# Smaller batches for the overflow slots of a mixture of experts, one branch for its general path, and an earlier place for it

## The chip, the cores and the metric

The kernel runs on one core of one Trainium2 chip. The metric is the device time of one execution in microseconds (us), as the median over several runs; lower is better.

## The reference, cut to what matters

Two blocks run one after the other on 256 tokens of 1024 values, all in float32. The first has a gated linear attention layer with a dense feed-forward layer, then a stick-breaking attention layer with a mixture of experts; the second has two hybrid attention layers. The change lies in the mixture of experts:

```python
def moe_swiglu(h, w_router, w_gate, w_up, w_down):
    logits = (h @ w_router).astype(jnp.float32)
    top_val, top_idx = lax.top_k(logits, TOP_K)          # 2 of 8
    top_w = jax.nn.softmax(top_val, axis=-1)
    gates = jnp.sum(jax.nn.one_hot(top_idx, N_EXPERTS) * top_w[..., None], axis=-2)
    out = jnp.zeros_like(h)
    for e in range(N_EXPERTS):
        y = (jax.nn.silu(h @ w_gate[e]) * (h @ w_up[e])) @ w_down[e]
        out = out + gates[..., e:e + 1] * y
    return out
```

`w_gate[e]` and `w_up[e]` are 1024 x 3584, `w_down[e]` is 3584 x 1024.

## The kernel before

The program is one instruction list for each engine, with no loops on the chip. A Python planner writes it: `spawn` and `after` put side work (generators) on a list, `tick` advances each by one step, and `until` and `drain` tick until a condition holds or until no side work is left. So the Python order is the order of each engine's queue.

**Weights.** `order` lists every weight chunk in order of use. `load_more` (L308) issues the next load on SP's queue (L322) for each slot in the list `free`; `let_go` (L333) puts the slots of used chunks back and calls `load_more`. A load waits on the chip until the last reader of its slot is done. In the mixture of experts there are 4 + 6 general slots, two named `extra`, and two more (`T..h`, `T..l`) that serve until the chunk `moe_g6_0_0` is reached in `order`: 14 in all, each for one chunk.

**Routing.** `route` computes the logits, ranks them, counts positions with small matmuls, sets `over_i` (has the expert more than 64 tokens?) and `most_i` (the largest count), builds the one-hot selection `pick` (`pick_pair`) and the scaled input `xs`, and `gather` then collects the tokens of two experts at a time into `xe`. TensorE also clears the bank `po` once before (L1404).

**Experts.** `moe_steps` has 16 steps, (e, g) for expert e and half g of its 3584 columns. Each expert has 64 slots for tokens, 32 further ones (`BEYOND`), and a general path for more. A step does `up` for the gate and for the up weights (8 chunks each), then `down` of the step before (7 chunks). A pass of `up` multiplies its 8 chunks by the 64 slots (L1240). Then `beyond` (L1213 on, the branch is at L1220) runs the same chunks for the 32 further slots (L1249) only if the expert's flag is set; the flag is a register on TensorE alone. Only after that are the 8 slots of the chunks let go. `down` does the same in batches of four and three (L1300, L1311). `scatter` adds the result to `X`, with matmuls for the further slots (L1199) in every case.

**General path.** `second(e2, first)` runs an expert for tokens past 96, with its own weight loads on SP. It stands in two branches (L1415), one for `first` 96 and one for 224, each over eight experts, ahead of step (6, 1). It is not taken with these inputs. It uses the two `T` slots as buffers, and `drain` runs ahead of it.

**After the last step**, `down` of step (7, 1) and its `scatter` start the norms of the hybrid layer (`TwoNorms`), and `pump` splits the first weight parts of that layer into a high and a low part (ScalarE L353, VectorE L359).

Of the kernel before, what the change touches and what calls it, by code (L numbers as in the profile page):

```python
# [16 lines left out]
P = 128  # L17
# [94 lines left out]
def whole(ctx, tc, T, out, tap):  # L112
# [919 lines left out]
    with tc.tile_pool(name="moe", bufs=1) as pool:  # L1032
# [23 lines left out]
        def route():  # L1056
            lp = yield from grab("y")
            for k in range(KT):
                while k // 4 not in norm.done:
                    yield  # L1060
                mm3(lp[0:NE, 0:S], sl(wr, ALL, k), sl(xT, ALL, k), k == 0, k == KT - 1)
                if k % 4 == 3:
                    yield
            lT = ring.tile([NE, S], F32, tag="wlo", name="lT", bufs=LA + 1)
            V.tensor_copy(lT, lp[0:NE, 0:S])
            for tt in range(2):
                nc.tensor.transpose(lp[:, S + tt * NE:S + (tt + 1) * NE], lT[:, toks(tt)], ident[0:NE, 0:NE])
            yield
            V.tensor_copy(flat(lg), lp[:, S:S + 2 * NE])
            drop(lp)  # L1070

            rank = pool.tile([P, 2, NE], F32, name="rank")
            gt, eq = (ring.tile([P, 2, NE, NE], F32, tag="wlo", name=n, bufs=LA + 1) for n in ("gt", "eq"))
            other = [lg[:, tt, :].unsqueeze(1).to_broadcast([P, NE, NE]) for tt in range(2)]
            mine = [lg[:, tt, :].unsqueeze(2).to_broadcast([P, NE, NE]) for tt in range(2)]
            for tt in range(2):
                V.tensor_tensor(eq[:, tt], other[tt], mine[tt], ALU.is_equal)
            for tt in range(2):
                V.tensor_tensor(gt[:, tt], other[tt], mine[tt], ALU.is_gt)
            V.tensor_mul(eq, eq, C("low").rearrange("p (a b) -> p a b", a=NE).unsqueeze(1).to_broadcast([P, 2, NE, NE]))  # L1080
            V.tensor_add(gt, gt, eq)
            V.tensor_reduce(rank, gt, AX.X, ALU.add)
            V.tensor_scalar(sel, rank, 2.0, None, op0=ALU.is_lt)
            yield
            ps = yield from grab("y")
            mm(ps[:, 0:NE], C("pos_tri"), sel[:, 0, :], start=True, stop=True)
            mm(ps[:, NE:2 * NE], C("pos_tri"), sel[:, 1, :], start=True, stop=False)
            mm(ps[:, NE:2 * NE], ones, sel[:, 0, :], start=False, stop=True)
            mm(ps[:, 2 * NE:3 * NE], ones, sel[:, 0, :], start=True, stop=False)
            mm(ps[:, 2 * NE:3 * NE], ones, sel[:, 1, :], start=False, stop=True)  # L1090

            over = pool.tile([P, NE], F32, name="over")
            V.tensor_scalar(over, ps[:, 2 * NE:3 * NE], SLOTS + 0.5, None, op0=ALU.is_gt)
            V.tensor_copy(over_i, over)
            counted.append(over_i)
            while not norm.ready:
                yield
            for tt in range(2):
                V.tensor_scalar(lg[:, tt, :], lg[:, tt, :], rstd[:, tt:tt + 1], None, op0=ALU.mult)
            for j in range(2):  # L1100
                for tt in range(2):
                    act(xs[0][:, tt, cols(j)], X[:, tt, cols(j)], AF.Copy, scale=rstd[:, tt:tt + 1])
                if j == 0:
                    V.tensor_copy(flat(pos), ps[:, 0:2 * NE])
                    pick_pair(0)
                else:
                    act(gates_, gates_, AF.Exp)
                for tt in range(2):
                    V.scalar_tensor_tensor(xs[1][:, tt, cols(j)], X[:, tt, cols(j)], rstd[:, tt:tt + 1], xs[0][:, tt, cols(j)], ALU.mult, ALU.subtract)
                if j == 0:  # L1110

                    top = pool.tile([P, 2], F32, name="top")
                    V.tensor_reduce(top, lg, AX.X, ALU.max)
                    V.tensor_tensor(gates_, lg, top.unsqueeze(2).to_broadcast([P, 2, NE]), ALU.subtract)
                    spawn(gather(0, 1))
                yield

            most = pool.tile([P, 1], F32, name="most")
            V.tensor_reduce(most, ps[:, 2 * NE:3 * NE], AX.X, ALU.max)
            drop(ps)  # L1120
            V.tensor_copy(most_i, most)
            yield 2
            V.tensor_mul(gates_, gates_, sel)
            gsum = pool.tile([P, 2], F32, name="gsum")
            V.tensor_reduce(gsum, gates_, AX.X, ALU.add)
            V.reciprocal(gsum, gsum)
            V.tensor_mul(gates_, gates_, gsum.unsqueeze(2).to_broadcast([P, 2, NE]))
# [51 lines left out]
        def scatter(e, y, z, nxt, ring_):  # L1179
# [8 lines left out]
            for tt in range(2):  # L1188
# [3 lines left out]
                    pbs[tt, half] = take_bank(ring_)  # L1192
                for half in range(2):
                    r = slice(half * 64, half * 64 + 64)
                    mm(pbs[tt, half], pT[r, 0, toks(tt)], ys[r, :], start=True, stop=False)
                for i in range(2):
                    for half in range(2):
                        r = slice(half * 64, half * 64 + 64)
                        mm(pbs[tt, half][:, i * 256:i * 256 + 256], pT[r, 1 + i, toks(tt)], zs[r, :], start=False, stop=i == 1)  # L1199
                yield  # L1200
                if not nxt:
                    for half in range(2):
# [23 lines left out]
        def up(e, g, n):  # L1226


            xe = xes[e // 2]
            c0 = e % 2 * P  # L1230
            mine, more_ = slice(c0, c0 + SLOTS), slice(c0 + SLOTS, c0 + SLOTS + BEYOND)
            pss = [bank("w"), bank("w")]
            ws = []
            for k in range(KT):
                until(lambda: done_k.get(e // 2, 0) > k)
                ws.append(chunk_at(f"moe_{n}{e}_{g}_{k}"))
                w_ = ws[-1][1][:, 0, :]
                for ps, a, b in ((pss[0], 0, 512), (pss[1], 512, QUART)):
                    for half in range(2):
                        mm(ps[half * 64:half * 64 + 64, 0:b - a], xe[:, k, mine], w_[:, half * QUART + a:half * QUART + b],  # L1240
                           start=k == 0, stop=k == KT - 1)
                tick()
            until(lambda: not in_po)
            in_po.append((e, g, n))

            def work():
                for k, (_, w_) in enumerate(ws):
                    for q in range(4):
                        mm(po[q * 32:q * 32 + 32, :], xe[:, k, more_], w_[:, 0, QCOL[q]:QCOL[q] + 512], start=k == 0, stop=k == KT - 1)  # L1249
            beyond(e, work)  # L1250
            let_go(i for i, _ in ws)
            tick()
            return pss

        hTs, ys, scattered = {}, {}, set()
# [68 lines left out]
        def second(e, first):  # L1324
# [21 lines left out]
            for g in range(ED // 512):  # L1346
                gu = []
                for ww in ("moe_w_gate", "moe_w_up"):
                    o = bank("fg")
                    for c in range(2):  # L1350
                        wf = raw_weights([P, 4, 512])
                        nc.sync.dma_start(wf, chunk(T[ww][0, e], c * 512, 4, g * 512, 512))
                        for kk in range(4):
                            mm(o, x2[:, c * 4 + kk, :], wf[:, kk, :], start=c + kk == 0, stop=c * 4 + kk == KT - 1)
                    gu.append(o)
# [7 lines left out]
                V.tensor_copy(flat(hT), ps)  # L1363
                for c in range(2):
                    wf = raw_weights([P, 2, D])
                    nc.sync.dma_start(wf, chunk(T["moe_w_down"][0, e], g * 512 + c * 256, 2, 0, D))
                    for kk in range(2):
                        for half in range(2):
                            i = c * 2 + kk
# [30 lines left out]
        spawn(route(), 0)  # L1400
        tick()
        po, in_po = bank("o"), []
        for q in range(4):
            mm(po[q * 32:q * 32 + 32, :], zeros, X[:, 0, 0:512], start=True, stop=True)  # L1404

        until(lambda: 0 in xes)
        free.extend((cpool, f"T{(t_at[0] + 1) % 2}{x}", order.index("moe_g6_0_0")) for x in "hl")
        load_more()
        prev = None
        for e, g in moe_steps:  # L1410
            if (e, g) == (NE - 2, 1):
                drain()
                most_v = nc.values_load(most_i[0:1, 0:1], min_val=0, max_val=S)
                for first in (SLOTS + BEYOND, SLOTS + BEYOND + P):
                    with tc.If(most_v > first):  # L1415
                        for e2 in range(NE):
                            second(e2, first)
            if (e, g) == (NE - 1, 0):
                spawn(spread_gain())
            if g == 0 and e % 2 and e < NE - 1:  # L1420
# [56 lines left out]
        rings["l"], ring_at["l"] = [7, 4, 5, 6], 0  # L1477
        norm = TwoNorms(cpool, [hT0], "n", [fg], DELAYS["hyb0"])
        down(*prev, norm.start)
        until(lambda: NE - 1 in scattered)  # L1480
        pump(st["pos"])
    more.close()
    if tap("moe", X):
        return
# [352 lines left out]
```

## Time and profile before

| | |
|---|---|
| median of 3 runs | 2048.58 us (2047.46 to 2048.61) |
| profiled execution, its own time | 2047.97 us |
| its span | 2046.2 us |
| TensorE busy in the span | 1944.7 us |
| HBM read | 532.91 MB |

The profile is of one execution. The span runs from the first to the last instruction; 1.8 us lie around it. The mixture of experts takes the span from about 424 to 1345 us. Rows name an engine, a line of the kernel and a tile; PE is TensorE, PEld its weight load, DVE VectorE, ACT ScalarE, SP the engine that issues the loads; a name with q is the engine's own sequencer.

### The profile page before, as it was taken

What the parts mean: (1) busy time and instruction counts of PE and PEld (TensorE: products, weight loads), DVE (VectorE), ACT (ScalarE), POOL (GpSimd) and SP (SyncE); (2) the same over time, 40 slices, a digit from 0 to 9 for tenths busy, and PEclk for the clock granted to TensorE, in tenths of its full rate; (3) what the DMA queues carried; (4) which work ended last, traced back from release to release, by engine and by line L of the source; (5) the groups of instructions that cost most, each with busy time, mean ns of one, the idle gap of its engine ahead of it and who ended that gap; (6) DMA issues with size and microseconds to landing.
All of it is one profiled execution on the core that took longest, in us unless ns stands there. A gap on an engine that the chain in (4) does not pass through costs nothing. (4 is left out here: it accounts for less than half of the span.)

```text
span 2046.2 us, 27694 instructions
## 1 busy us (share of the span) xinstructions
PE 1944.7 (95%) x11238; PEld 1245.4 (61%) x11238; DVE 840.1 (41%) x1678; ACT 671.4 (33%) x1161; POOL 3.7 (0%) x11
## 2 busy tenths in 40 slices
PE   8999999988888889999999899889999999999998
PEld 7889999953233223443333333267877888787886
DVE  5665557631010101010100102065677666667765
ACT  5554446530000000000010000055565645556553
POOL 0000000000000000000000000000000000000000
PEclk9999999989999999999999899999999999999999
DMA  7486554329999999999997599974444555444552
GB/s 239 137 287 210 190 186 163 127 102 416 418 417 419 417 417 408 390 373 416 417 410 302 230 408 385 391 246 141 140 144 150 180 185 168 141 145 138 171 177 80
DMA packets 179685, 536.22 MB, mean 262 GB/s; under 512 B 11186, under 2 KB 52530, under 8 KB 179524
## 3 DMA queue, kind: packets, MB, share of 16 engines
q1 hardware_dynamic: 175392, 531.66, 68.7%
q10 hardware_dynamic: 4132, 2.33, 0.5%
q8 instruction: 111, 1.82, 0.4%
q14 instruction: 50, 0.41, 0.1%
HBM read 532.91 MB, written 1.05 MB: 261 GB/s over the span
## 5 line engine op out<-in xcount | busy, mean ns | idle before, releaser
L359 DVE TENSOR_TENSOR wlo<-raw,whi 128x1024 fp32r<-128x1024 f32 x338 | 412.8, 1224 | 273.1 <-PE psw L387 125.0
L353 ACT CAST whi<-raw 128x1024 fp32r<-128x1024 f32 x338 | 354.0, 1049 | 376.9 <-PE psw L388 239.8
L1240 PE MATMUL psw<-raw,xe 128*64 128x512 f32 (+1 forms) x2048 | 413.9, 548 | 42.7 <-DMA raw<-in_moe_w_up_dram 15.7
L1240 PEld LDWEIGHTS psw<-raw,xe 128*64 128x64 f32 x2048 | 142.8, 137 | 304.4 <-issue 218.0
L386 PE MATMUL psw<-whi,T0h 128*128 128x512 f32 (+1 forms) x784 | 315.5, 402 | 0.8 <-ACT T0h L448 0.8
L388 PE MATMUL psw<-whi,T0l 128*128 128x512 f32 (+1 forms) x784 | 304.4, 388 | 1.5 <-DVE T0l L450 1.5
L387 PE MATMUL psw<-wlo,T0h 128*128 128x512 f32 (+1 forms) x784 | 304.4, 388 | 0.0
L1300 PE MATMUL psy<-raw,hT 128*64 128x512 f32 x896 | 209.7, 601 | 22.3 <-DMA raw<-in_moe_w_down_dram 21.5
L1269 DVE TENSOR_TENSOR s<-s,psw 128x512 f32<-128x512 f32 x16 | 11.0, 688 | 442.2 <-issue 252.9
L386 PEld LDWEIGHTS psw<-whi,T0h 128*128 128x128 f32 x784 | 147.5, 188 | 39.9 <-issue 9.3
L388 PEld LDWEIGHTS psw<-whi,T0l 128*128 128x128 f32 x784 | 147.4, 188 | 35.8 <-DVE T0l L450 1.9
L387 PEld LDWEIGHTS psw<-wlo,T0h 128*128 128x128 f32 x784 | 147.8, 188 | 28.5
L1300 PEld LDWEIGHTS psy<-raw,hT 128*64 128x64 f32 x896 | 57.9, 136 | 146.4 <-issue 91.9
L386 PE MATMUL psw<-T1h,whi 128*128 128x256 f32 x432 | 122.7, 284 | 1.5 <-ACT whi L353 1.5
L388 PE MATMUL psw<-T1h,wlo 128*128 128x256 f32 x432 | 121.7, 282 | 0.5 <-DVE wlo L359 0.5
L387 PE MATMUL psw<-T1l,whi 128*128 128x256 f32 x432 | 121.5, 281 | 0.0
L1283 ACT COPY hT<-pss 128x384 f32<-128x384 f32 x16 | 7.7, 478 | 330.0 <-PE pss L1281 248.9
L1261 ACT ACTIVATE s<-psw 128x512 f32<-128x512 f32 x16 | 9.6, 597 | 305.5 <-PE psw L1240 305.5
L1249 PE MATMUL pso<-raw,xe 128*32 128x512 f32 x768 | 84.9, 594 | 0.0
L386 PEld LDWEIGHTS psw<-T1h,whi 128*128 128x128 f32 x432 | 81.8, 189 | 3.8 <-ACT whi L353 2.7
L388 PEld LDWEIGHTS psw<-T1h,wlo 128*128 128x128 f32 x432 | 82.9, 192 | 0.8 <-DVE wlo L359 0.8
L387 PEld LDWEIGHTS psw<-T1l,whi 128*128 128x128 f32 x432 | 81.8, 189 | 0.4
(376 smaller groups left out, 2210.6 us busy)
## 6 DMA issues: line engine op xcount, KB each, us to landing
raw<-in_moe_w_gate_dram SPq DMA_DIRECT2D x128, 896.0 KB, 17.4
raw<-in_moe_w_up_dram SPq DMA_DIRECT2D x128, 896.0 KB, 14.9
raw<-in_moe_w_down_dram SPq DMA_DIRECT2D x112, 1024.0 KB, 16.9
raw<-in_w_in_dram SPq DMA_DIRECT2D x80, 1024.0 KB, 5.0
raw<-in_gla_w_in_dram SPq DMA_DIRECT2D x11, 1024.0 KB, 8.5
raw<-in_ffn_w_gate_dram SPq DMA_DIRECT2D x11, 1024.0 KB, 5.3
raw<-in_ffn_w_up_dram SPq DMA_DIRECT2D x11, 1024.0 KB, 5.5
raw<-in_ffn_w_down_dram SPq DMA_DIRECT2D x11, 1024.0 KB, 5.2
```

The lines of the kernel that those rows point to most:

```text
L353: A.copy(his[i], part_of(i))
L359: V.tensor_sub(los[i], part_of(i), his[i])
L386: mm(o, a[0], b[0], start=start, stop=False)
L387: mm(o, a[0], b[1], start=False, stop=False)
L388: mm(o, a[1], b[0], start=False, stop=stop)
L1240: mm(ps[half * 64:half * 64 + 64, 0:b - a], xe[:, k, mine], w_[:, half * QUART + a:half * QUART + b], start=k == 0, stop=k == KT - 1)
L1249: mm(po[q * 32:q * 32 + 32, :], xe[:, k, more_], w_[:, 0, QCOL[q]:QCOL[q] + 512], start=k == 0, stop=k == KT - 1)
L1261: act(s[:, 0:512], pss[0], AF.Silu)
L1269: V.tensor_mul(s[:, 0:512], s[:, 0:512], pss[0])
L1283: (A.copy if i % 2 else V.tensor_copy)(flat(dst), pb[:, 0:n * P])
L1300: mm(y[half * 64:half * 64 + 64, :], hT[:, i, h * 64:h * 64 + 64], ws[-1][1][:, a, cols(half)], start=(g, c, a) == (0, 0, 0), stop=(g, c, ...
```

## The change

- A pass of `up` runs the branch for the further slots after every four chunks (after every two in the very first pass) and lets their slots go then, where it was once after eight.
- `scatter` puts the matmuls for the further slots into the branch.
- The general path stands ahead of step (2, 1), with one branch around both values of `first`, and its loads are issued from ScalarE's queue. The two `T` slots join the list of free slots only behind it, and serve until `moe_g7_1_0`.
- `route` copies the positions and builds `pick` ahead of the wait for the norm; `over_i` is computed at the end.
- `po` is cleared four ticks later.
- `pump` behind the last step is gone; one high and one low part are made ahead of the last `scatter`, the others come with the first projection.

```diff
@@ route
-            over = pool.tile([P, NE], F32, name="over")
-            V.tensor_scalar(over, ps[:, 2 * NE:3 * NE], SLOTS + 0.5, None, op0=ALU.is_gt)
-            V.tensor_copy(over_i, over)
-            counted.append(over_i)
+            V.tensor_copy(flat(pos), ps[:, 0:2 * NE])
+            pick_pair(0)
             while not norm.ready:
                 yield
...
-                if j == 0:
-                    V.tensor_copy(flat(pos), ps[:, 0:2 * NE])
-                    pick_pair(0)
-                else:
+                if j:
                     act(gates_, gates_, AF.Exp)
...
+            over = pool.tile([P, NE], F32, name="over")
+            V.tensor_scalar(over, ps[:, 2 * NE:3 * NE], SLOTS + 0.5, None, op0=ALU.is_gt)
+            V.tensor_copy(over_i, over)
+            counted.append(over_i)
@@ scatter
-                    mm(pbs[tt, half], pT[r, 0, toks(tt)], ys[r, :], start=True, stop=False)
-                for i in range(2):
-                    for half in range(2):
-                        r = slice(half * 64, half * 64 + 64)
-                        mm(pbs[tt, half][:, i * 256:i * 256 + 256], pT[r, 1 + i, toks(tt)], zs[r, :], start=False, stop=i == 1)
+                    mm(pbs[tt, half], pT[r, 0, toks(tt)], ys[r, :], start=True, stop=True)
+
+                def work():
+                    for i in range(2):
+                        for half in range(2):
+                            r = slice(half * 64, half * 64 + 64)
+                            mm(pbs[tt, half][:, i * 256:i * 256 + 256], pT[r, 1 + i, toks(tt)], zs[r, :], start=False, stop=True, skip_group_check=True)
+                beyond(e, work)
@@ up
-            ws = []
-            for k in range(KT):
...
-            until(lambda: not in_po)
-            in_po.append((e, g, n))
...
-            beyond(e, work)
-            let_go(i for i, _ in ws)
-            tick()
+            step = 2 if (e, g, n) == (0, 0, "g") else 4
+            for k0 in range(0, KT, step):
+                ws = []
+                for k in range(k0, k0 + step):
...
+                if k0 == 0:
+                    until(lambda: not in_po)
+                    in_po.append((e, g, n))
...
+                beyond(e, work)
+                let_go(i for i, _ in ws)
+                tick()
@@ second, for the gate and up weights and for the down weights
-                        nc.sync.dma_start(wf, ...)
+                        A.dma_start(wf, ...)
@@ the steps
-        for q in range(4):
-            mm(po[q * 32:q * 32 + 32, :], zeros, X[:, 0, 0:512], start=True, stop=True)
+        def clear_po():
+            for q in range(4):
+                mm(po[q * 32:q * 32 + 32, :], zeros, X[:, 0, 0:512], start=True, stop=True)
+        after(4, clear_po)
         until(lambda: 0 in xes)
-        free.extend((cpool, f"T{(t_at[0] + 1) % 2}{x}", order.index("moe_g6_0_0")) for x in "hl")
-        load_more()
         prev = None
         for e, g in moe_steps:
-            if (e, g) == (NE - 2, 1):
+            if (e, g) == (2, 1):
                 drain()
                 most_v = nc.values_load(most_i[0:1, 0:1], min_val=0, max_val=S)
-                for first in (SLOTS + BEYOND, SLOTS + BEYOND + P):
-                    with tc.If(most_v > first):
+                with tc.If(most_v > SLOTS + BEYOND):
+                    for first in (SLOTS + BEYOND, SLOTS + BEYOND + P):
                         for e2 in range(NE):
                             second(e2, first)
+                free.extend((cpool, f"T{(t_at[0] + 1) % 2}{x}", order.index(f"moe_g{NE - 1}_1_0")) for x in "hl")
+                load_more()
@@ behind the last step
         down(*prev, norm.start)
+        hi_next()
+        lo_next()
         until(lambda: NE - 1 in scattered)
-        pump(st["pos"])
```

## Rows read from the trace of the kernel before

**Rows 1.** The page: TensorE's busy time, and GB/s moved in 40 equal slices.
```profile
PE 1944.7 (95%) x11238; PEld 1245.4 (61%) x11238; DVE 840.1 (41%) x1678; ACT 671.4 (33%) x1161; POOL 3.7 (0%) x11
...
GB/s 239 137 287 210 190 186 163 127 102 416 418 417 419 417 417 408 390 373 416 417 410 302 230 408 385 391 246 141 140 144 150 180 185 168 141 145 138 171 177 80
```

**Rows 2.** Windows cut at TensorE's gate-pass branches: busy us by engine, clock, DMA share, GB/s.
```profile
442.40:457.90 15.50, 15.34 (x83) 6.54 (x83) 0.00 (x0) 4.53 (x9) 0.00 (x0) 0.97 0.00 1
...
483.50:536.90 53.40, 44.35 (x213) 13.20 (x211) 4.21 (x9) 2.05 (x4) 0.00 (x0) 1.00 1.02 417
...
750.10:806.40 56.30, 55.02 (x341) 19.60 (x339) 9.26 (x18) 2.54 (x5) 0.00 (x0) 1.00 1.02 417
806.40:870.30 63.90, 63.90 (x475) 25.38 (x473) 3.28 (x5) 5.51 (x12) 0.00 (x0) 1.00 0.96 383
870.30:921.00 50.70, 49.45 (x337) 20.87 (x335) 9.17 (x18) 2.43 (x5) 0.00 (x0) 1.00 0.93 378
921.00:970.20 49.20, 44.12 (x221) 15.45 (x219) 4.22 (x9) 2.05 (x4) 0.00 (x0) 1.00 1.02 416
970.20:1026.40 56.20, 54.95 (x341) 19.54 (x339) 9.26 (x18) 2.53 (x5) 0.00 (x0) 1.00 1.02 417
1026.40:1090.40 64.00, 64.00 (x475) 25.45 (x473) 3.28 (x5) 5.52 (x12) 0.00 (x0) 1.00 0.91 366
1090.40:1167.20 76.80, 66.91 (x465) 24.94 (x463) 9.54 (x18) 2.53 (x5) 0.00 (x0) 0.91 0.73 290
1167.20:1226.70 59.50, 59.50 (x443) 21.65 (x441) 3.27 (x5) 2.16 (x4) 0.00 (x0) 1.00 0.92 369
1226.70:1281.70 55.00, 52.10 (x341) 19.98 (x339) 10.54 (x20) 2.42 (x5) 0.00 (x0) 1.00 0.95 382
1281.70:1336.00 54.30, 45.75 (x217) 14.41 (x213) 3.27 (x6) 2.05 (x4) 0.00 (x0) 1.00 0.96 381
```

**Rows 3.** Waits of SP's queue: us in total, times, longest.
```profile
SPq L322 <- PEq L1220: 159.9, 23, 27.0
```

**Rows 4.** DMA issues: KB each, median us from issue to landing.
```profile
raw<-in_w_in_dram SPq DMA_DIRECT2D x80, 1024.0 KB, 5.0
```

**Rows 5.** Timeline of SP around the first pass: start, length, what.
```profile
424.04 6.71 SPq L322 DMA_DIRECT2D raw<-in_moe_w_up_dram  x4
...
457.85 0.80 SPq L322 DMA_DIRECT2D raw<-in_moe_w_up_dram  x2
```

**Rows 6.** Timeline of PE, parts of experts 2 to 4: idle before in brackets.
```profile
716.77 1.08 PE L1300 MATMUL psy<-raw,hT 128*64 128x512 f32 x4 [0.88 <-DMA raw<-in_moe_w_down_dram]
...
758.04 12.25 PE L1240 MATMUL psw<-raw,xe 128*64 128x512 f32 x64
770.21 7.07 PE L1249 MATMUL pso<-raw,xe 128*32 128x512 f32 x64
777.22 5.37 PE L1300 MATMUL psy<-raw,hT 128*64 128x512 f32 x24
...
873.73 1.08 PE L1240 MATMUL psw<-raw,xe 128*64 128x512 f32 x4 [0.31 <-PEq L1220]
```

**Rows 7.** Lines L1220 and L1415 alone: ns min/median/max, first and last start.
```profile
L1220 PEldq COMPARE_BRANCH  x88: 65/181/442, 455.0 to 1334.0; - x88
...
L1415 SPq EVENT_SEMAPHORE  x16: 17/17/17, 1153.7 to 1157.5; - x16
...
L1415 PEldq COMPARE_BRANCH  x2: 4817/5443/6069, 1143.4 to 1149.6; - x2
```

**Rows 8.** Timeline of PE behind the general path.
```profile
1154.76 5.91 PE L1240 MATMUL psw<-raw,xe 128*64 128x512 f32 x16 [9.89 <-PEq L1415]
```

**Rows 9.** Timeline of the routing: the clearing of po, and the first picks.
```profile
425.21 1.06 PE L1404 MATMUL pso<-X,zeros 128*32 128x512 f32 x8
...
436.84 1.12 DVE L1054 TENSOR_SCALAR pick<-consts,pos,sel 128x128 fp32r<-128x128 f32 x4
```

**Rows 10.** Timeline of PE at the start of the hybrid layer.
```profile
1347.57 0.50 PE L388 MATMUL psw<-whi,T0l 128*128 128x512 f32 x1 [1.48 <-DVE T0l L450]
```

More of the change, by code (lines that the diff above doesn't have):

```diff
@@ L1232, in up, with work @@
             pss = [bank("w"), bank("w")]
-            ws = []
-            for k in range(KT):
[L1235 to L1241, printed above, removed]
-                tick()
-            until(lambda: not in_po)
-            in_po.append((e, g, n))
-            def work():
-                for k, (_, w_) in enumerate(ws):
-                    for q in range(4):
-                        mm(po[q * 32:q * 32 + 32, :], xe[:, k, more_], w_[:, 0, QCOL[q]:QCOL[q] + 512], start=k == 0, stop=k == KT - 1)
-            beyond(e, work)
-            let_go(i for i, _ in ws)
-            tick()
+            step = 2 if (e, g, n) == (0, 0, "g") else 4
+            for k0 in range(0, KT, step):
+                ws = []
+                for k in range(k0, k0 + step):
+                    until(lambda: done_k.get(e // 2, 0) > k)
+                    ws.append(chunk_at(f"moe_{n}{e}_{g}_{k}"))
+                    w_ = ws[-1][1][:, 0, :]
+                    for ps, a, b in ((pss[0], 0, 512), (pss[1], 512, QUART)):
+                        for half in range(2):
+                            mm(ps[half * 64:half * 64 + 64, 0:b - a], xe[:, k, mine], w_[:, half * QUART + a:half * QUART + b],
+                               start=k == 0, stop=k == KT - 1)
+                    tick()
+                if k0 == 0:
+                    until(lambda: not in_po)
+                    in_po.append((e, g, n))
+                def work():
+                    for i, (_, w_) in enumerate(ws):
+                        k = k0 + i
+                        for q in range(4):
+                            mm(po[q * 32:q * 32 + 32, :], xe[:, k, more_], w_[:, 0, QCOL[q]:QCOL[q] + 512], start=k == 0, stop=k == KT - 1)
+                beyond(e, work)
+                let_go(i for i, _ in ws)
+                tick()
             return pss
@@ L1351, in second @@
                         wf = raw_weights([P, 4, 512])
-                        nc.sync.dma_start(wf, chunk(T[ww][0, e], c * 512, 4, g * 512, 512))
+                        A.dma_start(wf, chunk(T[ww][0, e], c * 512, 4, g * 512, 512))
                         for kk in range(4):
@@ L1365, in second @@
                     wf = raw_weights([P, 2, D])
-                    nc.sync.dma_start(wf, chunk(T["moe_w_down"][0, e], g * 512 + c * 256, 2, 0, D))
+                    A.dma_start(wf, chunk(T["moe_w_down"][0, e], g * 512 + c * 256, 2, 0, D))
                     for kk in range(2):
@@ L1402, in whole @@
         po, in_po = bank("o"), []
-        for q in range(4):
-            mm(po[q * 32:q * 32 + 32, :], zeros, X[:, 0, 0:512], start=True, stop=True)
+        def clear_po():
+            for q in range(4):
+                mm(po[q * 32:q * 32 + 32, :], zeros, X[:, 0, 0:512], start=True, stop=True)
+        after(4, clear_po)
         until(lambda: 0 in xes)
-        free.extend((cpool, f"T{(t_at[0] + 1) % 2}{x}", order.index("moe_g6_0_0")) for x in "hl")
-        load_more()
         prev = None
         for e, g in moe_steps:
-            if (e, g) == (NE - 2, 1):
+            if (e, g) == (2, 1):
                 drain()
                 most_v = nc.values_load(most_i[0:1, 0:1], min_val=0, max_val=S)
-                for first in (SLOTS + BEYOND, SLOTS + BEYOND + P):
-                    with tc.If(most_v > first):
+                with tc.If(most_v > SLOTS + BEYOND):
+                    for first in (SLOTS + BEYOND, SLOTS + BEYOND + P):
                         for e2 in range(NE):
                             second(e2, first)
+                free.extend((cpool, f"T{(t_at[0] + 1) % 2}{x}", order.index(f"moe_g{NE - 1}_1_0")) for x in "hl")
+                load_more()
             if (e, g) == (NE - 1, 0):
```

## The prediction

> **What bounds the kernel now.** I read the page first. TensorE is busy for 95% of the span, yet the line of GB/s has two levels: about 140 to 290 outside the mixture of experts and some 417 in most of it, with dips in slices 16 to 18, 21, 22, 24 and 25 [rows 1]. So the mixture has two possible bounds, and I cut it into windows at the branch of each gate pass to see which holds where [rows 2]. In step (0, 1) (five windows alike from 483.5 to 750.1) the loads run at 417 GB/s without a pause while TensorE has gaps: the loads are the bound. A step loads 16 chunks of 0.917 MB and 7 of 1.049 MB, 22.0 MB, which is 52.7 us at 417.5 GB/s. From 750.1 on TensorE is nearly full and the loads pause, except in step (4, 1). An expert whose flag is set (3, 5 and 6) takes TensorE 56 to 64 us a step, the others less than the loads need. The two limits alternate, and each is lost time only while the other's buffer is empty or full. Setting GB/s against 417.5, the loads stand still for 15.5 us in the first window, 5.3 + 4.8 in the next two dips, 7.9 + 23.4 + 6.9 + 4.7 around experts 5 to 7 and 4.7 at the end.
>
> Then I asked what SP waits for. The largest wait behind a branch of `up` is 27.0 us [rows 3]: a load waits for a slot, and a slot comes free only when eight chunks are through. That is the first pass: SP issues four loads at 424 and the next at 457.85 [rows 5].
>
> **The change part by part.**
>
> *First pass.* The first window has eight chunks in 15.5 us [rows 2], 1.94 each. After two chunks, at 442.4 + 3.9 = 446.3, slots now come free; the register load and one skip add some, the routing takes some off. I take 445.5 against 457.85, 12.3 us sooner. But the `T` slots aren't in use yet, so 12 chunks are loaded by then and not 14: two chunks at 2.2 us are lost. Gain 8 us, which the stretch bound by loads passes on whole; from 4 (release 4 us later) to 10.
>
> *Routing.* Clearing `po` (1.06 us) and `pick` (1.12 us) leave the chain to the first gather [rows 9]; at most 2.2 us, at least 0, counted inside the 8.
>
> *Branches.* Five experts skip. Each gets four more skips in `up` and two in `scatter`, and the first pass two more: 32. A skip costs the sequencer 65 to 442 ns [rows 7], and TensorE runs dry before the next matmul for 0.31 us where data is there and up to 0.88 us where a load is waited for as well [rows 6]. So 10 to 28 us in all. Most lie in steps where a step of loads (52.7 us) covers 43 us of TensorE's, so they are free there; if that cover were gone they would all count. Eight to twelve lie in steps (4, 0) to (4, 1) and (7, 0) to (7, 1), which I expect TensorE to bound: 12 x 0.31 = 3.7, less the matmuls that `scatter` no longer does. I take 2.5, and nothing for the taken branches.
>
> The Trainium skill (Runtime: NRT & Kernel Launch, Instruction fetch mechanics) says that a taken branch whose target lies outside the window of fetched pages stalls for a DMA fetch. The long jumps of L1415, 4.8 and 6.1 us on TensorE, agree; the jumps of L1220, at most 0.44 us, don't show it, so the sum goes by those.
>
> *General path.* Before, it stops TensorE for 9.89 us, and the next 16 matmuls take 5.91 us where 64 take 12.25 afterwards at the full clock [rows 6, 8], so 2.8 us more: some 12.7 us, in a step that TensorE bounds. After, one jump of 5 to 6 us stands in a step bound by loads. TensorE may stop there as long as loads go on: 12 chunks are then loaded or under way, 26 us of work, against a stop of about 6 us for the jump and the drained side work (I allow 8). What can stop the loads is the catching up of semaphores: SP has 16 of these instructions at L1415, eight a branch [rows 7], one set for the loads that weren't issued. They move to ScalarE with the loads. I take it that each waits for the loads ahead of it, so SP's next load starts once all in flight have landed: one empty pipe. A lone 1 MB load lands in 5.0 us [rows 4], of which 2.5 are transfer at 417 GB/s; so 2.5, and I take 3 us. The other end is what the stop cost the loads before: 23.4 us in that window less the 9.3 by which its 62 us exceed 52.7, 14 us. Behind ScalarE's wait stands the gate activation of step (2, 1); it feeds `down` of that step, one step (50 us) later.
>
> *Slots let go by four.* In a pass of eight, loads can be 14 - 8 = 6 chunks ahead when slots come free, and 4 for loads of expert 6, where the two `T` slots have left; now 14 - 4 = 10. From step (3, 0) on I go by steps, TensorE against loads. TensorE alone: 56.3, 63.9, 50 for (3, 0) to (4, 0) from [rows 2]; (4, 1) has no flag and no wait for data, 56.3 - 2 x 7.07 [rows 6] = 42.2 plus skips, 43; then 56.2 and 64.0; (6, 0) is 76.8 - 12.7 = 64, its like (6, 1) 59.5, I take 62 and 59.5; (7, 0) 53; the last window two passes of `down` at 7 x 1.79 and one of `up` at 12.25, 37.3 plus 6 for the rest, 43. The sum is 551 against 585.9 before. The lead of the loads, in us and starting at 2: 5.6, 16.8, 14, 4.3, 7.8, 19.1, then 28 and 35 but for the limit of ten chunks (22 us), and still 15 to 20 at the last step, which needs 53 of loads against 55 of TensorE: just enough. So TensorE bounds all of it: 35 us less, 32.5 after the skips. If the lead gets no farther than six chunks, only the stop and a few us go: 14.
>
> *End.* `pump` no longer holds VectorE ahead of the first `T0l`, for which TensorE waits 1.48 us [rows 10]; but one split now stands ahead of the last copy of `y`. Between -1.5 and +1.5 us, I take 0.5. The hybrid layers behind are shifted as they are.
>
> Sum: 8 - 3 + 32.5 + 0.5 = 38 us. The profiled execution took 2047.97 us (span 2046.2 and 1.8 around it), 0.6 below the median, so 2010 for the median.
>
> **The rivals.**
>
> *A second stop.* The stop of the loads moves with the branch, at its old price of 14 us in a stretch bound by loads. For it: jumps are slow, and ScalarE catches up only after its own jump and the drain. Against it: SP no longer jumps, and 26 us of loads are under way. 2010 + 11 = 2021.
>
> *Six chunks stay the limit,* because SP, TensorE or the slots lag in a way that the count of slots doesn't show: 8 - 3 + 14 = 19, so 2029. For it: the loads pause for 10.1 us in windows 806 to 921 [rows 2], where a limit of six chunks (13.2 us) should leave 3.6 of a lead of 16.8.
>
> *No pause of the loads at all.* The pauses from 442 on sum to 73 us; if TensorE's steps hide more waits than I read off and ten more us come back, 1998.
>
> *The skips decide, slower.* TensorE is 95% busy [rows 1]. If it is the bound throughout, earlier loads bring nothing, the stop shrinks by 9.89 - 6 = 4 us at most, and 32 skips at 0.31 to 0.88 us cost 10 to 28: about 2063 with 19. Against it: TensorE's gaps in five windows at 417 GB/s. It decides from 38 / 32 = 1.2 us a skip. If each extra jump cost what the shorter jump of L1415 does, 4.8 us, it would be 154 us slower; 1%, since 88 jumps and falls-through of L1220 are in the trace and none took over 0.44 us. That is the rule of the Trainium skill named above, taken to the letter.
>
> **How the numbers follow.** The forecast has 0.55 (its own range 2002 to 2018); the second stop 0.14, six chunks 0.12, no pause 0.10; the skips 0.06, of which 0.01 the far jumps; no change 0.03, if gains and skips cancel. The range takes in the first four but for their outer ends: 1996 to 2029. 0.2% (4 us) is about what a measurement of this kernel can tell from no change. Faster 0.91, same 0.03, slower 0.06.
>
> **What would show it.** Right: SP's loads resume at about 445; one stop at step (2, 1), TensorE idle there but GB/s dipping for some 3 us only; SP without semaphore instructions at the branch; GB/s at 417 through window 806 to 921; the last two experts with TensorE full and pauses of the loads about 7 us each in expert 6; the hybrid layer beginning near 1300. Wrong: a dip of 10 us or more behind the branch; idle TensorE at 0.5 us or more behind each new skip in steps where loads are not the bound; waits of TensorE for `raw` in experts 5 and 6, which would mean that the lead is not there.

## The result and the profile after

The changed kernel took 2022.46 us (median of 4 runs, 2019.51 to 2024.0) against 2048.02 of the kernel before on the same chip: a ratio of 0.9874, 95% interval 0.9857 to 0.9891. It is 25.6 us faster where the prediction said 38; the forecast of 2010 was 12 us too low, inside its range. The profiled execution took 2023.1 us, 24.9 less than the one of before.

The page's line of GB/s after, against [rows 1]: counted from 1, the dips in slices 16 to 18 are gone, one has come up in slice 14, which was at 417, and those in slices 22 to 25 stay.

```profile
PE 1936.7 (96%) x11158; PEld 1244.8 (62%) x11158; DVE 839.8 (42%) x1678; ACT 671.5 (33%) x1161; POOL 3.7 (0%) x11
...
GB/s 242 133 288 208 188 189 169 126 122 416 416 415 416 366 417 418 417 413 417 417 416 377 315 378 374 405 200 133 139 146 157 177 187 168 142 129 146 167 187 73
```

Windows of the kernel after, with the columns of [rows 2]: the first pass, step (0, 1), the stretch behind the general path, and steps from (3, 0) on, cut at the last branch of each gate pass (the stretch behind the general path from the first one there). The first row is the kernel before, for the second.

```profile
424.80:442.40 17.60, 11.19 (x61) 7.93 (x58) 11.01 (x47) 6.51 (x15) 0.00 (x0) 0.74 0.60 220
424.80:442.40 17.60, 12.01 (x61) 7.64 (x61) 11.08 (x47) 7.29 (x17) 0.00 (x0) 0.71 0.28 112
442.40:457.90 15.50, 14.46 (x78) 6.52 (x76) 0.00 (x0) 3.95 (x7) 0.00 (x0) 1.00 0.64 246
488.60:530.10 41.50, 37.43 (x185) 13.47 (x181) 4.20 (x9) 0.48 (x1) 0.00 (x0) 1.00 1.02 414
...
692.90:749.10 56.20, 51.80 (x273) 18.18 (x275) 5.32 (x11) 2.06 (x4) 0.00 (x0) 1.00 0.93 374
749.10:806.30 57.20, 55.49 (x333) 18.22 (x331) 9.24 (x18) 2.54 (x5) 0.00 (x0) 1.00 1.02 417
806.30:866.80 60.50, 60.34 (x438) 23.94 (x436) 3.28 (x5) 5.53 (x12) 0.00 (x0) 1.00 1.02 415
866.80:918.90 52.10, 50.55 (x340) 21.45 (x338) 9.17 (x18) 2.43 (x5) 0.00 (x0) 1.00 1.02 417
...
1085.20:1150.60 65.40, 64.61 (x469) 23.56 (x467) 9.26 (x18) 2.54 (x5) 0.00 (x0) 1.00 0.87 338
1150.60:1206.60 56.00, 55.84 (x407) 20.14 (x405) 3.28 (x5) 2.17 (x4) 0.00 (x0) 1.00 0.93 372
1206.60:1261.40 54.80, 54.19 (x343) 21.72 (x341) 10.64 (x20) 2.54 (x5) 0.00 (x0) 0.97 0.93 376
1261.40:1309.30 47.90, 44.56 (x217) 16.09 (x213) 3.26 (x6) 2.06 (x4) 0.00 (x0) 1.00 1.02 407
```

The ends of these windows can't be set against those of [rows 2] one by one: TensorE's sequencer passes a branch ahead of the products (the last one of the gate pass of (3, 0) at 749.05 in after, its products end at 751.8), and at the last branch of a gate pass half of the products for the further slots are now done already. So the gain is followed along the mixture by products that both kernels have. Before, then after: the first product of `down` in steps (2, 0) and (2, 1) ([rows 6] has the latter of before, at 716.77), and the last chunk of `down` in the mixture.

```profile
662.66 1.94 PE L1300 MATMUL psy<-raw,hT 128*64 128x512 f32 x8 [0.84 <-DMA raw<-in_moe_w_down_dram]
1334.03 1.94 PE L1300 MATMUL psy<-raw,hT 128*64 128x512 f32 x8 [0.63 <-DMA raw<-in_moe_w_down_dram]
```
```profile
657.39 1.94 PE L1306 MATMUL psy<-raw,hT 128*64 128x512 f32 x8 [0.84 <-DMA raw<-in_moe_w_down_dram]
716.31 1.94 PE L1306 MATMUL psy<-raw,hT 128*64 128x512 f32 x8 [0.58 <-DMA raw<-in_moe_w_down_dram]
1307.40 1.94 PE L1306 MATMUL psy<-raw,hT 128*64 128x512 f32 x8 [0.78 <-DMA raw<-in_moe_w_down_dram]
```

The kernel after is 5.3 us ahead in step (2, 0), 0.5 us in step (2, 1) and 26.6 us at the last chunk. The hybrid layer then starts its third product at 1323.48 against 1347.57 [rows 10], a gain of 24.1. So 5.3 was won in the first pass, 4.8 lost at the general path, 26.2 won from there to the end of the mixture, 2.5 lost behind it. What lies between 24.1 and the 24.9 of the whole execution is in the layers behind, which the change doesn't touch.

*The first pass.* SP's first load behind it goes out at 447.02 us, against 457.85 [rows 5]:

```profile
447.02 0.80 SPq L322 DMA_DIRECT2D raw<-in_moe_w_up_dram  x2
```

In the window from 442.4 to 457.9, in which nothing was loaded before [rows 2], 246 GB/s flow. The window ahead of it has 112 GB/s where it had 220: without the two `T` slots two chunks fewer are loaded ahead.

*The general path.* The line of its branch alone (count, ns min/median/max, first and last start), and SP's waits (us, times, longest):

```profile
L1420 SPq EVENT_SEMAPHORE  x8: 17/17/17, 700.4 to 700.9; - x8
...
L1420 PEldq COMPARE_BRANCH  x1: 6120/6120/6120, 680.4 to 680.4; - x1
...
L1420 ACTq EVENT_SEMAPHORE  x1: 17/17/17, 681.9 to 681.9; - x1
L1420 SPq COMPARE_BRANCH  x1: 50/50/50, 683.9 to 683.9; - x1
```
```profile
SPq L322 <- PEq L1222: 163.9, 39, 22.7
...
SPq L1420 <- SPq L1420: 16.4, 1, 16.4
```

SP passes its branch at 683.9 and gets to its eight semaphores at 700.4. Its last load was issued at 682.5 and landed at 700.35, 0.02 us ahead of the first of the eight; the next goes out at 701.31. The loads are on ScalarE's queue now, yet the eight semaphores have stayed with SP, and ScalarE has one. From 692.9 to 749.1 the loads run at 374 GB/s instead of 417: 56.2 x 43 / 417 = 5.8 us of loading lost. TensorE's own stop is 7.09 us, and its first 16 products run at a granted clock of 0.58 for 5.46 us:

```profile
686.84 5.46 PE L1244 MATMUL psw<-raw,xe 128*64 128x512 f32 x16 [7.09 <-PEq L1420]
```

*The end.* TensorE around the last scatter, then ScalarE, then VectorE there:

```profile
1313.12 2.08 PE L1194 MATMUL psl<-ys,pickT 64*128 64x512 f32 x4 [3.78 <-DVE ys L1181]
1315.35 2.08 PE L1194 MATMUL psl<-ys,pickT 64*128 64x512 f32 x4 [0.16 <-PEq L1222]
```
```profile
1310.16 1.04 ACT L353 CAST whi<-raw 128x1024 fp32r<-128x1024 f32 x1 [23.04 <-DMA raw<-in_w_in_dram]
1311.11 0.37 ACT L1182 COPY zs<-psz 128x256 f32<-128x256 f32 x1
```
```profile
1311.24 1.23 DVE L359 TENSOR_TENSOR wlo<-raw,whi 128x1024 fp32r<-128x1024 f32 x1 [22.67 <-ACT whi L353]
1312.38 0.68 DVE L1181 COPY ys<-psy 128x512 f32<-128x512 f32 x1
```

The split of the next weights stands ahead of the copy of `y` on both engines, and it waits for `w_in`'s chunk. So the last scatter starts 3.78 us after the last product of `down`, which ends at 1309.34.

### The profile page after: what moved, and what is told of

Its sections match the earlier page's. It is cut to its first block, busy times and chain, and to the rows that moved or that the text cites. A ratio compares the mean times of both kernels' runs of the same rounds, so it can differ in the third digit from the quotient of the medians.

```text
span 2021.3 us, 27618 instructions
## 1 busy us (share of the span) xinstructions
PE 1936.7 (96%) x11158; PEld 1244.8 (62%) x11158; DVE 839.8 (42%) x1678; ACT 671.5 (33%) x1161; POOL 3.7 (0%) x11
## 5 line engine op out<-in xcount | busy, mean ns | idle before, releaser
L1244 PEld LDWEIGHTS psw<-raw,xe 128*64 128x64 f32 x2048 | 148.9, 138 | 290.1 <-issue 220.0
L1306 PE MATMUL psy<-raw,hT 128*64 128x512 f32 x896 | 208.0, 600 | 14.7 <-DMA raw<-in_moe_w_down_dram 13.4
L1275 DVE TENSOR_TENSOR s<-s,psw 128x512 f32<-128x512 f32 x16 | 11.0, 687 | 457.9 <-PE psw L1244 232.8
```

The costliest lines, as they stand in the source:

```text
L1306: mm(y[half * 64:half * 64 + 64, :], hT[:, i, h * 64:h * 64 + 64], ws[-1][1][:, a, cols(half)], start=(g, c, a) == (0, 0, 0), stop=(g, c, ...
```

## The experiments

Each kernel was timed beside the kernel before on its own chip; the three medians of before there (2047.59 for e1 to e4, 2047.57 for e5 to e8, 2047.97 for e9 to e12) agree with 2048.02, so times are set against the 2022.46 of the kernel after. Against it, the intervals separate e1, e5, e9 and e12 only; the others lie within 5.1 us of it and overlap, so for them the traces have to show where the difference arises.

| kernel | us | ratio to before, 95% interval |
|---|---|---|
| after | 2022.46 | 0.9874 (0.9857 to 0.9891) |
| e1 batches of eight | 2036.55 | 0.9948 (0.9935 to 0.9962) |
| e2 general path at (6, 1) | 2027.14 | 0.9897 (0.9882 to 0.9912) |
| e3 its loads on GpSimd | 2017.86 | 0.9856 (0.9841 to 0.9872) |
| e4 copies before casts | 2017.36 | 0.9856 (0.9841 to 0.9871) |
| e5 three edits | 2006.12 | 0.9799 (0.9786 to 0.9813) |
| e6 picks late | 2025.45 | 0.9891 (0.9876 to 0.9906) |
| e7 scatter without skip | 2026.28 | 0.9895 (0.9880 to 0.9910) |
| e8 batches of two | 2026.44 | 0.9900 (0.9885 to 0.9915) |
| e9 e5, slots to the end | 2004.09 | 0.9787 (0.9774 to 0.9801) |
| e10 its loads on SP | 2022.29 | 0.9872 (0.9857 to 0.9887) |
| e11 first pass by four | 2025.42 | 0.9891 (0.9876 to 0.9906) |
| e12 before, loads on GpSimd | 2048.42 | 1.0003 (0.9993 to 1.0012) |

**The stop of the loads: e3, e10, e12.** My theory after reading the trace was that SP waits for its own newest load, because the semaphores that it must catch up are those which its loads use.

```diff
-                        A.dma_start(wf, ...)            # e3: the kernel after
+                        nc.gpsimd.dma_start(wf, ...)    # e10: nc.sync; e12: in before
```

> The kernel after, with the loads of the branch not taken issued on GpSimd's queue instead of ScalarE's; nothing else. Their semaphores are then others than those of SP's loads, and SP has nothing of them to catch up on when it passes the branch. Theory: SP's stop of 16.4 us at the branch is the wait for its own newest load in flight, since the semaphores it must catch up are those its loads use; without it loads go on, about 5.8 us of transfers come back, and all of the steps up to (4,1) that the loads bound are earlier by that: 2018 us (2016 to 2020). Rival: the stop is that of taking the branch (its flag, its code), and moving the loads changes nothing: 2022 (2021 to 2024).

> The kernel after with the loads of the branch not taken issued by SP again; nothing else. Theory: moving them to ScalarE brought nothing, since SP catches up on the same eight semaphores in both cases and waits for its own newest load; what SP does more is one longer jump, inside that wait: 2022.5 us (2021 to 2024.5). Rival: SP's jump over the loads comes on top, as TensorE's does: 2026 or more.

> The kernel before, with the loads of its two branches not taken on GpSimd's queue; nothing else. Theory: the waits of 12.2 and 2.6 us of SP at the branches of (6,1) are the same wait for its own loads and go away; TensorE's own stop of 9.9 us stays, and the loads were at the limit of their slots in these steps, so little is gained: 2045 us (2042 to 2047.5). Rival: SP's stop was what the step cost, and the time falls by 8 or more: below 2040.

e3 brought 4.6 us, as expected; in its trace it is 4.5 us ahead of after from step (3, 0) on (first product of `down` at 770.24 and 774.75). Its branch has no semaphores on SP any more; GpSimd does the catching up, at 443 us, when nothing hangs on it. The same window as above then has the loads at full rate:

```profile
L1420 POOLq EVENT_SEMAPHORE  x4: 17/43/43, 443.3 to 443.5; - x4
```
```profile
692.90:749.10 56.20, 55.28 (x308) 20.76 (x310) 5.32 (x11) 3.15 (x6) 0.00 (x0) 1.00 1.02 417
```

e10 is the kernel after within the measurement, with the same wait, so the move to ScalarE's queue did nothing:

```profile
SPq L1420 <- SPq L1420: 16.1, 1, 16.1
```

e12 ended 0.9 us above my expected range, and no faster than before: the two waits of SP at the branches (14.8 us in all in the kernel before, 12.2 the longest) are gone in it as well, and nothing is gained. There TensorE stood still for 9.9 us itself and the loads were at the limit of their slots. The same wait of SP cost nothing that can be measured at (6, 1) and 4.6 us at (2, 1), where the loads are the bound.

**Where the general path stands: e2.**

```diff
-            if (e, g) == (2, 1):       # one If; T slots after it
+            if (e, g) == (NE - 2, 1):  # two Ifs, loads on SP; T slots from the start to (6, 0)
```

> The kernel after with the general path put back to the seventh expert's second step, with two branches and its loads on SP, and the two slots given from the start until (6,0); batches of four, early picks and end stay. Theory: the stop at (2,1) costs about 5 us of load time and goes away, two more slots in the first pass let two more loads run ahead (up to 4 us); at (6,1) TensorE stands for 10 us as before and SP for over 10 us, with eight chunks of lead: about equal, 2022 us (2016 to 2030). Rival: the early place is worth the whole difference between the two stops: 2030 or more. Other rival: the early place loses more than it gains: below 2016.

4.7 us slower than after, inside the expected range. Several things change at once in e2, and the trace takes them apart: it is 5.0 us ahead before step (2, 1), from the two more slots in the first pass, and 9.9 behind it, since there is no stop. Then TensorE stands still in a step that it bounds, and the mean granted clock of the step is 0.91. The step takes 80.2 us where after has 65.40, 14.8 more:

```profile
1075.30:1155.50 80.20, 69.42 (x469) 25.30 (x467) 9.53 (x18) 2.54 (x5) 0.00 (x0) 0.91 0.72 278
```
```profile
1137.28 1.94 PE L1244 MATMUL psw<-raw,xe 128*64 128x512 f32 x3 [9.96 <-PEq L1423]
```

**The size of the batches: e1, e8, e11.**

```diff
-            step = 2 if (e, g, n) == (0, 0, "g") else 4
+            step = 2 if (e, g, n) == (0, 0, "g") else KT    # e1; e8: 2; e11: 4
```

> The kernel after with gate and up passes in one batch of eight chunks again (the very first gate pass stays in four batches of two); the general path at (2,1) and its slots, the early picks and the end stay. Theory: batches of four are what the steps from (3,0) on gained, since a slot comes back after four chunks and not after eight; of the 25.6 us all is lost but the first pass (about 6.5), less the 5 of the general path, plus a little for the two slots that here stay until the last step: 2043 us (2038 to 2050). Rival: the gain came from those two slots, which before were taken away at (6,0): then 2022 to 2030.

> The kernel after with all gate and up passes in batches of two: 12 chunks of lead instead of 10, and two more branches in every pass but one (64 in all, some 40 of them skips). Theory: in the stretch that TensorE bounds the lead of ten is enough and each skip costs 0.15 to 0.5 us: 4 to 8 us slower, 2028 us (2024 to 2032). Rival: the lead still binds, as it did with eight (e1): faster than 2020.

> The kernel after with the very first gate pass in batches of four as well, instead of two. Theory: SP's first load then waits for four chunks and not two, two chunks of 1.94 us later; the loads bound the stretch behind it and up to (3,0), so that they pass on what the pipe of loads lost, less what a later pause gives back: 2024.5 us (2023 to 2026.5). Rival: the first pass is bound by the gather and the loads, and its own batches don't matter: 2022.5.

e1 lost 14.1 us, not the 20 and more that I expected: the batches are worth about 14 of the 25.6, and my share for them was too large. The gain of the first pass needs them too: in e1 the gate pass of (1, 0) ends 5.5 us later than in after, since SP gets the eight loads of the first pass out early, as after does, and then waits for all eight chunks of the up pass (next load at 470.34, against 463.98 in after). At the end TensorE waits for every chunk of the last `down` (idle before in brackets; one of seven such rows):

```profile
1306.80 1.94 PE L1306 MATMUL psy<-raw,hT 128*64 128x512 f32 x8 [0.71 <-DMA raw<-in_moe_w_down_dram]
```

It also shows the price of a branch that is taken. Expert 5's step (5, 1) is TensorE's alone in both kernels (first e1, then after), and two branches more cost 0.6 us:

```profile
1033.00:1096.20 63.20, 63.20 (x471) 25.02 (x471) 3.28 (x5) 5.48 (x12) 0.00 (x0) 1.00 0.95 383
```
```profile
1025.20:1089.00 63.80, 63.80 (x471) 24.65 (x475) 3.29 (x5) 5.50 (x12) 0.00 (x0) 1.00 0.98 394
```

e8 agrees. From the end of `down` of (4, 0) to that of (6, 0), where all passes of gate and up take the branch, it has 16 branches more and takes 248.6 us against 244.6 (first after, then e8), 0.25 us each:

```profile
950.50:1195.10 244.60, 241.79 (x1662) 86.86 (x1664) 25.08 (x46) 12.77 (x26) 0.00 (x0) 1.00 0.95 380
```
```profile
954.20:1202.80 248.60, 245.79 (x1662) 83.96 (x1664) 25.09 (x46) 12.75 (x26) 0.00 (x0) 1.00 0.92 366
```

As a whole e8 is 4.0 us slower: ten chunks of lead are enough, and more branches only cost. They cost more than the whole shows: the last product of the mixture ends at 1316.72, 7.4 us later than in after, and some 5.6 come back behind it, where TensorE is idle for 1.62 us ahead of the last scatter and not 3.78. e11 is 3.0 us slower, as expected: SP's first load goes out at 449.81 instead of 447.02, and of these 2.8 us 2.6 are still there at the last product of the mixture (1311.9 against 1309.3).

**The end: e4.**

```diff
         down(*prev, norm.start)
+        tick()
         hi_next()
         lo_next()
```

> The kernel after, with one turn of the queues before the two casts of the next weights at the end, so that the last scatter's two copies out of PSUM stand ahead of them on VectorE and ScalarE; nothing else. Theory: TensorE's 3.78 us idle before the last scatter is the wait for the copies behind the casts, which wait for w_in's chunk; it falls to about 0.8 as before: 2019.5 us (2018.5 to 2020.5). Rival: the casts are then late for the first product after the norm and take the 3 us back: 2022 to 2023.

5.1 us faster, beyond the range that I gave. The idle time falls to 0.80, and the scatter's products take 1.13 us instead of 2.08:

```profile
1309.39 1.13 PE L1194 MATMUL psl<-ys,pickT 64*128 64x512 f32 x4 [0.80 <-DVE ys L1181]
1310.68 1.13 PE L1194 MATMUL psl<-ys,pickT 64*128 64x512 f32 x4 [0.16 <-PEq L1222]
```

Between the last product of the mixture and the third of the hybrid layer lie 9.5 us instead of 14.1, so 4.7 of the 5.1 are there. What is more than the idle time is the clock. Windows of the scatter, after and then e4: behind 3.78 us of idle TensorE the granted clock is 0.50, the lower of its two levels (1.2 GHz); behind 0.80 us it stays at 1.00.

```profile
1313.10:1317.40 4.30, 4.12 (x8) 1.04 (x8) 0.75 (x1) 0.00 (x0) 0.00 (x0) 0.50 0.72 267
```
```profile
1309.40:1311.80 2.40, 2.24 (x8) 0.62 (x8) 1.37 (x2) 0.99 (x1) 0.00 (x0) 1.00 1.05 387
```

The Trainium skill (TensorE: Matmul & The Clock Gate, Part 1) says that the clock is set by how busy the array has been of late; these two windows agree. The part of the clock isn't the same in every execution: of eight traces with 3.6 to 3.8 us of idle TensorE here, six have 0.50 over these products, e2 has 0.66 and e1 0.77.

**Small parts: e6, e7.**

```diff
-            V.tensor_copy(flat(pos), ps[:, 0:2 * NE])   # e6: behind the first casts of xs again,
-            pick_pair(0)                                #     the count ahead, po cleared first
```
```diff
-                beyond(e, work)    # e7: the products of zs always run
+                work()
```

> The kernel after with the routing in the old order again (the clearing of po ahead of the routing, picks behind the first casts of xs, the count of the overfull experts ahead of them). Theory: the first gather starts up to 2 us later, and so does the first freed slot; the loads bound what follows and pass it on: 2024 us (2022.5 to 2025). Rival: the early picks are what lets the loads start again 11 us sooner: 2027 or more.

> The kernel after, with scatter's products of zs outside the branch, as before. Theory: it is worth little: two skips fewer an expert (0.16 to 0.9 us of TensorE idle each) against 8 small products more a group (1.03 us) in the five experts that skip; three of those five lie where the loads bound: within 1.5 us of 2022.5. Rival, that skips are dear: below 2020; rival, that they save much: above 2025.

They came out slower by 3.0 us (0.45 beyond its range) and 3.8 us. In the profile of e6 SP's first load goes out at 447.76, 0.74 us later, which is all that I can point to; whether the early picks are worth 1 or 3 us stays open. e7 missed its range of 1.5 us: the skip in the scatter saves more than I gave it. In its trace the last `down` ends 1.4 us later than in after, and the hybrid layer's third product starts 3.7 us later (1327.16 against 1323.48); the last scatter, whose products of `zs` run at the lower clock there, takes 5.49 us instead of 4.31.

**All of it together: e5, e9.** The third edit of e5 gives the two `T` slots from the start until (2, 1) as well as after the general path; e9 keeps them for the whole mixture.

```diff
         until(lambda: 0 in xes)
+        free.extend(... order.index("moe_g2_1_0") ...)          # e5, with e3 and e4
+        load_more()
...
-                free.extend(... order.index(f"moe_g{NE - 1}_1_0") ...)
+                free.extend(... past_moe ...)                   # e9
```

> The kernel after with three edits: the branch's loads on GpSimd's queue (as e3), one turn of the queues before the last two casts (as e4), and the two T slots given from the start of the mixture until the chunk of (2,1), as well as after the general path. Theory: the three act at different places and add up: 4.6 (e3), 5.1 (e4), and the third brings what e2 showed up to (2,0), 5 us, since the stretch up to there is bound by the loads and two more chunks can run ahead at the start: 2022.5 - 14.7 = 2008 us (2005 to 2011). Rival: with loads earlier by 10 us TensorE is the bound sooner, and the third or the first is lost: 2012 to 2014.

> The kernel of e5, with the two T slots kept for all chunks of the mixture instead of those ahead of (7,1); nothing else. Theory: in the last step the loads have 12 slots and not 14, so they pause behind it and the last four chunks of down are waited for (0.53 to 0.65 us each in e5, 2.4 us in all); with two more chunks ahead (5 us of loads) these waits go: 2003.7 us (2003 to 2005). Rival: the last chunks are late because of the rate of the loads or of the pause of the step before, and two slots more change nothing: 2006.

2006.12 and 2004.09 us: the edits add up, as expected (16.3 us in e5 where the sum was 14.7). In e9 the last `down` runs without a wait for a chunk (first row: behind the skip; second: the last three chunks), where after lost 0.33 to 0.78 us ahead of each of the last four:

```profile
1282.67 7.09 PE L1306 MATMUL psy<-raw,hT 128*64 128x512 f32 x32 [0.40 <-PEq L1222]
1289.91 5.39 PE L1306 MATMUL psy<-raw,hT 128*64 128x512 f32 x24 [0.15 <-PEq L1222]
```

e9 is faster than both kernels, 18 us below the kernel after.

## Why the prediction was right in its direction and 12 us off in size

By its own sum, in us, each term from the products set against each other above:

| step | predicted | measured |
|---|---|---|
| first pass | +8 | +5.3 |
| general path | -3 | -4.8 |
| slots by four, less skips | +32.5 | +26.2 |
| end | +0.5 | -2.5 |
| sum to the hybrid layer | +38 | +24.1 |

*First pass: right in mechanism and within its 4 to 10 us.* SP's loads were said to resume at 445.5; they did at 447.02. The two chunks that the missing `T` slots cost are seen in the window at 112 GB/s, and e5 and e9 got them back (218 and 220 GB/s there, and 5.3 and 4.7 us ahead of after in step (2, 0)).

*General path: the step that failed is "They move to ScalarE with the loads".* The semaphores stayed with SP (eight, at 700.4), and with them the wait of 16.4 us; e3 prices it at 4.6 of the 4.8, and e10 shows that the queue which the change chose makes no difference. I had called the time of one empty pipe 3 us. By the window it is 5.8. My rival of a second stop gave 2021 and the time came out near it, but not by its mechanism: it had ScalarE late, and at 14 us. That TensorE's stop of 7 us is hidden at (2, 1) was right: e3 has it and e2 doesn't, and e2 is 5.3 us ahead of e3 before it (first product of `down` in step (2, 0) at 652.37 and 657.64) and 5.4 us behind it (in step (3, 0) at 764.82 and 770.24).

*Slots by four: the mechanism holds, the size was 6 us too large.* The loads go on at 415 and 417 GB/s through (3, 1) and (4, 0), where they paused before [rows 2], and nothing of TensorE's waits for `raw` in experts 5 and 6; so six chunks are no longer the limit. Two terms were mis-sized. I took "nothing for the taken branches": experts 3, 5 and 6 have 12 more of them, at 0.25 to 0.30 us (e8, e1), 3.0 to 3.6 us. And I found the lead at the last step "just enough": I had left out that the `T` slots, which come back with the change, leave again ahead of (7, 1); the last `down` takes 16.2 us in after and 13.2 in e9. Together these make up about the 6 us, though no run shows that the other terms of this sum were right one by one. And what I booked under this term is in good part something else: e1 shows that the batches are worth 14 us altogether, first pass included, and the stop taken out of (6, 1) is worth 12.1 in that step (from the first product of `down` in (6, 0) to that in (6, 1) 77.45 us before and 65.35 after; I had 12.7, and e2 loses 14.8). One part of the gain I hadn't thought of: in the gate pass of (3, 0) TensorE now runs half of the products for the further slots while it waits for the chunks that are left, where all 64 stood behind the last chunk. From the pass's first product to that of the up pass it takes 21.37 us instead of 23.78. Before, then after:

```profile
751.03 7.07 PE L1249 MATMUL pso<-raw,xe 128*32 128x512 f32 x64
```
```profile
741.98 3.64 PE L1255 MATMUL pso<-raw,xe 128*32 128x512 f32 x32
```

*End: the wrong sign.* I took 0.5 for a split that "now stands ahead of the last copy of `y`", by its own duration. I didn't ask what the split waits for. It waits for a chunk of `w_in` that came 0.8 us behind TensorE's last product (the cast starts at 1310.16, the product ended at 1309.34); then come 1.04 us of cast and 1.23 of subtraction before the copy, and behind the longer idle time the clock fell. e4 prices this at 5.1 us.

*Short branches: right that none stalls.* The branch for the further slots (`beyond`) is in the trace 156 times and none takes over 437 ns. The Trainium skill's rule on far targets (Runtime: NRT & Kernel Launch, Instruction fetch mechanics) agrees with the 6.12 us of the long jump at L1420, and no row of the short ones shows it.

*Two slips.* The dips that I named are in slices 16 to 18, 22, 23, 25 and 26 if all are counted from 1. And 2010 less ten more us is 2000, not the 1998 of the rival with no pause. Neither bears on the sum.

## What to carry to other kernels

A stall has no price of its own: TensorE's stop cost 12 to 15 us where TensorE was the bound and 0.2 us where the loads were, and SP's wait at the same branch the other way round, nothing that can be measured at one place and 4.6 at the other. When a branch with transfers in it is moved, look which queue catches up on their semaphores, and put them on one that has nothing under way. When an instruction is moved ahead of another on its engine, ask what it waits for, and not only how long it runs.

## What the runs showed that I had not expected

With the loads of the branch not taken on ScalarE's queue, SP did eight semaphore catch-ups and ScalarE one; with them on SP's own queue SP waits as long (16.1 us); with them on GpSimd's queue SP did none, and GpSimd did four. And 3.78 us of idle TensorE were enough to bring the granted clock to 0.50 for the next 4.3 us, which added 1.9 us to eight products; in e1, after 3.77 us, the first four of them still ran at the full clock (1.13 us) and the next four took 1.78.
